# Eight kilobytes of gather scratch turned into a seventh raw buffer and a seventh gather buffer, with one more U tile beside each of two copies

## The chip, the core and the metric

The kernel runs on one core of a Trainium2 chip. That core has a matrix engine (TensorE, PE in the rows below), a vector engine (VectorE, DVE), a scalar engine (ScalarE, ACT), a general engine (GpSimd, POOL) and an engine that mostly issues transfers (SyncE, SP), and it moves data with 16 DMA engines that all of its queues share. The metric is the device time in microseconds of one execution, the median of several runs.

## What is computed

One layer of a streaming encoder on 512 tokens of width 1024: two gated token mixers, then a channel mixer called PEER, in which each token picks 128 of 16384 single-neuron experts (8 heads, 16 experts a head) and adds up their outputs. All of it is float32. The part that this study touches is the second one:

```
q = (t @ w_q).reshape(n_tok, PEER_HEADS, 2, PEER_HALF)
sc = jnp.einsum("thpk,hpnk->thpn", q, sub_keys)          # scores against 2 x 128 keys a head
s_top, i_top = lax.top_k(sc, PEER_TOPK)                  # 16 best of each half, then 16 best sums
...
ue = u_tab[ib]                                           # 128 rows of U for each token
act = jax.nn.gelu(jnp.einsum("phkd,pd->phk", ue, tb))
ve = v_tab[ib]                                           # and 128 rows of V
return jnp.einsum("phk,phkd->pd", gb * act, ve)
```

## The kernel before

The first 360 us are the token mixers (56 weight tiles against all 512 tokens), the next 200 us the queries, scores and top-16 selections. From there PEER is done in two ways at once.

**Tokens 128 to 511 (three token tiles) go the dense way.** The 16384 rows of U are 128 "U tiles" of 128 rows. For each U tile `h_mm` multiplies it with the three token tiles: 24 matmuls of 384 columns, since each float32 operand is split into a high part `hi_u` (made by ACT) and a low part `lo_u` (made by DVE or POOL), and three of the four products are taken. ACT then applies gelu and leaves `hg`, 128 x 384. The gates of the chosen experts are turned into a dense 16384 x 384 matrix by one-hot matmuls (`pg`) that ACT writes to a tile `stg`, 64 KB a partition, one token tile at a time. There is one `stg` buffer. So after token tile 0 and after token tile 1 it is copied out to DRAM (`gd`, four transfers of 2 MB each, line 777), and the one-hot matmuls of the next token tile can only be written once the copy has ended. The third token tile's gates stay in `stg`. In the last phase, iteration i (0 to 127) loads V tile i, reads back the gates `gt` (from `gd`), multiplies them with `hg` to weights `wf`, splits both operands, and adds 18 matmuls of 512 columns to six accumulators (`acc`, lines 831 to 835).

**Tokens 0 to 127 go the sparse way.** POOL gathers 128 rows of U and then 128 rows of V by indirect DMA (`ru`, `rv`, 512 KB each); DVE makes one dot product or one weighted sum of each (lines 373 and 387). The index of a gather is released by ACT (`eix`, line 669), in iteration i of the last phase as a table `pace` says: about three an iteration while U tiles are still multiplied there, three in four iterations afterwards. 8 of the 256 gathers are done before the last phase.

**Where the U tiles are multiplied.** U tiles can run ahead of the last phase: 60 of them do (`nlag = SPILL + AHEAD`), spread by `HST` over the query phase, and then one in each step of the one-hot phase, and `HB` gives the extra steps that follow each copy's start. They are the work that PE has while `stg` is being copied out. 54 of the 60 results do not fit on the chip and are written to DRAM (`hd`, from ACT's queue) and read back as `hr`. The other 68 U tiles are multiplied in the last phase, one an iteration, in iterations 0 to 67; 60 iterations with V alone follow.

**Order.** Up to the last phase each engine's order but SP's is that of the source (`pinned`). In the last phase and on SP a scheduler orders the instructions by its own model of when each can start; only `eix` and gathers are held in source order. SP issues loads in one queue, in order: a load whose buffer is not yet free holds up those behind it. `raw` (U, V, W tiles as loaded, 4 KB a partition) is a ring of RB buffers, and the last four loads, `raw_x2s` (the residual rows that the result is added to), take buffers of the same ring. The gathers alternate between two pools of GR and DR buffers.

```
while t_ < NDT - 1 and len(raws) < RB:      # before a copy: fill the ring
    h_load()
...
for m in range(HB[t_]):                     # U tiles beside the copy
    h_step(lambda: None)
...
gather_release(pace[i], i)                  # ACT: the indices of this iteration's gathers
gather_steps(pace[i], GLEFT)                # POOL: the gathers; DVE: dot products but the last GLEFT
```

Of the kernel before, what the change touches and what calls it, by code (L numbers as in the profile page):

```python
# [35 lines left out]
CGROUPS = [(0, 1, 16), (1, 1, 8), (2, 1, 5), (3, 1, 4), (4, 1, 3), (5, 3, 2), (8, 8, 1)]  # L36
OC = 8
AHEAD = 6
SPILL = 54
OB = 2  # L40
HST = (0,) * 3 + (1,) * 14 + (2,) * 3
HB = (6, 6, 0)
HX = (14, 15, 16)
HPRE = 2
WARM = 28
# [1 line left out]
HPRO2 = 2  # L47
GSTEP = (1, 0, 0)
SB = 3
RB = 6  # L50
DR = 3
GTAIL = 0.5
LATE = 3
FP = (1, 2)
GLEFT = 3
GR = 3
TWO = ("xa", "xc", "cv", "hh", "yb", "gga", "sma")

# [2 lines left out]
def tile_block(ctx: ExitStack, tc: tile.TileContext, x, w_in, vecs, w_ax, w_out, n2row, w_q, skT,  # L61
# [36 lines left out]
    def load(src, name, nsub=None):  # L98
        raw = strm.tile([P, D], F32, tag="raw", name=f"raw_{name}", bufs=RB)
        dst = raw if nsub is None else raw.rearrange("p (a b) -> p a b", a=nsub)  # L100
        sync.dma_start(dst, src)
        return raw
# [273 lines left out]
    def drain(left):  # L376
        while len(dq) > left:
            dq.pop(0)()
# [23 lines left out]
    def h_act(i, pt):  # L402
        g = ha.tile([P, TD], F32, tag="hg", name=f"hg{i}", bufs=AHEAD)
        act.activation(g, pt[:, :TD], AF.Gelu_apprx_tanh)
        if i >= NKEY - SPILL:
            act.dma_start(hd[i - (NKEY - SPILL)], g)
        else:
            hg[i] = g

    def h_get(i):  # L410
        if i not in hg:
            hg[i] = ha.tile([P, TD], F32, tag="hg", name=f"hr{i}", bufs=AHEAD)
            sync.dma_start(hg[i], hd[i - (NKEY - SPILL)])
        return hg[i]

    hd = dram.tile([max(SPILL, 1), P, TD], F32, name="hd")
    hord = list(range(NKEY - SPILL, NKEY)) + list(range(NKEY - SPILL))
    nlag = SPILL + AHEAD
    gd = dram.tile([P, P, TG], F32, name="gd")
# [7 lines left out]
    def h_load():  # L427
        nonlocal hn
        if hn < nlag:
            raws.append((hord[hn], load(uT[hord[hn]], f"u{hord[hn]}")))  # L430
            hn += 1
# [226 lines left out]
    def gather_release(n, i):  # L658
        names, p = [], gpos[0]
        while len(names) < n and p < len(gsched):  # L660
            f, a = gsched[p]
            if f is not gather_w:
                names.append(("ru" if f is gather_u else "rv") + str(a))
            p += 1
        if names:
            t = dp.tile([P, 4], I32, tag="eix", name=f"eix{i}", bufs=4)
            for m, nm in enumerate(names):
                c = int(nm[2:])
                tc.keep_in_program_order(act.activation(t[:, m:m + 1], eall[:, 0, c:c + 1], AF.Copy))  # L669
                gidx[nm] = t[:, m:m + 1]  # L670

    def gather_steps(n, left=0):
        while n > 0 and gpos[0] < len(gsched):
            f, a = gsched[gpos[0]]
            f(a)
            drain(left)
            gpos[0] += 1
            if f is not gather_w:
                n -= 1
# [3 lines left out]
    with ExitStack() as gctx:  # L683
# [51 lines left out]
        def h_step(mid, splits=1):  # L735
            if len(raws) < RB:
                h_load()
            made = []
            while len(made) < splits and len(nxt) + len(made) < SB and raws:
                k_, raw = raws.pop(0)  # L740
                hi = strm.tile([P, D], F32R, tag="hi", name=f"hi_u{k_}", bufs=SB)
                act.activation(hi, raw, AF.Copy)
                made.append((k_, raw, hi))
            mid()
            for k_, raw, hi in made:
                lo = strm.tile([P, D], F32R, tag="lo", name=f"lo_u{k_}", bufs=SB)
                dve.tensor_tensor(lo, raw, hi, op=ALU.subtract)
                nxt.append((k_, (hi, lo), None))
            h_run()
            flush()  # L750
# [4 lines left out]
        for t_ in range(NDT):  # L755
            stg = sp.tile([P, P, P], F32, tag="stg", name=f"stg{t_}", bufs=1)
            for s2 in range(P // OC // 2):
# [8 lines left out]

                if s2 >= 3 and len(raws) < RB:
                    h_load()

                h_step(mid, 0 if t_ and s2 == 0 else 2 if s2 == 3 else 1)  # L770
                gather_steps(GSTEP[(sub // 2) % len(GSTEP)], 2)
            while t_ < NDT - 1 and len(raws) < RB:
                h_load()
            if t_ < NDT - 1:
                for q4 in range(4):
                    sl = slice(q4 * 32, (q4 + 1) * 32)
                    sync.dma_start(gd[sl, :, t_ * P:(t_ + 1) * P].rearrange("i j t -> j i t"), stg[:, sl, :])
            for m in range(HB[t_]):
                h_step(lambda: None)
# [8 lines left out]
    dp = ctx.enter_context(tc.tile_pool(name="dp", bufs=1))  # L788
    rpool.append((dp, DR))
    acc0 = dp.tile([P, D], F32, name="acc0")  # L790
# [49 lines left out]
    for i in range(NKEY):  # L840
# [20 lines left out]
        gather_release(pace[i], i)  # L861
        gather_steps(pace[i], GLEFT)
        if i == NKEY - LATE - 1:
            for j in range(i + 1, NKEY):
                vr[j] = load(v_tab[j * P:(j + 1) * P, :], f"v{j}")
            fgb = dp.tile([P, D], F32, tag="rows", name="fgb", bufs=DR)
            sync.dma_start(fgb, frow.partition_broadcast(P))
            x2s.extend(load(x2d[t], f"x2s{t}") for t in range(NTT))
            x2s.append(dp.tile([P, D], F32, tag="rows", name="junk", bufs=DR))
            drain(0)  # L870
# [51 lines left out]
```

## Time and profile before

| what | value |
|---|---|
| median of 3 runs | 1636.63 us (1634.88 to 1637.17) |
| the profiled execution, its own time | 1635.88 us |
| its span, first to last instruction | 1634.1 us, 1.8 us less than its time |
| PE busy | 1600.7 us, 98% |
| DVE, ACT, POOL busy | 1265.9, 687.7, 522.3 us |
| HBM traffic | 345.17 MB read, 31.59 MB written |
| DMA engines busy in the last phase | 0.93 of their time |
| granted TensorE clock, mean | 0.997 |

A row of a timeline gives the start in us from the span's start, the duration, the engine, the line of the kernel, the operation and the tiles (out<-in, buffer numbers left out), and in brackets how long the engine had been idle and what it had waited for. Matmuls overlap, so what one costs is the distance from its start to the next one's start, not its duration. A row of a stretch gives its ends and length in us, then the busy us and the number of instructions of PE, of PE's weight loads, of DVE, ACT and POOL, then the granted clock as a share of 2.4 GHz, the busy share of the DMA engines and GB/s. Waits are listed as who waited for whom: us in total, how many times, the longest.

### The profile page before, as it was taken

The page shows a single profiled execution, that of the slowest core. Times are in us where ns is not written, and L with a number is a line of the kernel's source. Part 1 is how long each engine was busy: PE and PEld are TensorE (multiplying, and loading weights), DVE is VectorE, ACT ScalarE, POOL GpSimd, SP SyncE. Part 2 cuts the span into 40 slices and gives each one's busy share as a digit, 9 for nine tenths or more (in the row PEclk, how much of TensorE's full clock was granted, in tenths as well). Part 3 has the DMA queues.
Part 4 walks back from the last instruction along what each step waited for, and adds up shares of the span by engine and source line. Part 5 has one row for each costly group of instructions (what it writes and reads, how often), then busy time and mean ns, then how long its engine had stood idle before and what let it go on. Part 6 is the DMA issues. An engine that isn't in the chain of part 4 may idle for free.

```text
span 1634.1 us, 23568 instructions
## 1 busy us (share of the span) xinstructions
PE 1600.7 (98%) x8402; PEld 1413.2 (86%) x8402; DVE 1265.9 (77%) x2404; ACT 687.7 (42%) x1222; POOL 522.3 (32%) x379
## 2 busy tenths in 40 slices
PE   9999999999999999998999999999999999999997
PEld 8888888888899999898989998898999888787775
DVE  6666666636999996767788878888888788877766
ACT  7444444434333454544433333333333333333334
POOL 0000000004788830000144444545444544223331
PEclk9999999999999999999999999999999999999999
DMA  6222222335332357787599989999999999988884
GB/s 227 94 93 94 94 94 96 99 106 180 111 120 101 126 192 221 264 251 232 188 316 333 337 315 329 326 336 319 349 330 335 326 327 348 323 305 297 284 301 144
DMA packets 157878, 378.31 MB, mean 232 GB/s; under 512 B 14016, under 2 KB 78016, under 8 KB 157632
## 3 DMA queue, kind: packets, MB, share of 16 engines
q1 hardware_dynamic: 112544, 229.86, 41.4%
q0 software_dynamic: 36864, 134.23, 23.3%
q10 hardware_dynamic: 8352, 12.72, 2.1%
q8 instruction: 65, 1.06, 0.3%
q14 instruction: 53, 0.43, 0.1%
HBM read 345.17 MB, written 31.59 MB: 231 GB/s over the span
## 4 chain that ended last, share of the span: by engine, by line
PE 59%; DMA 15%; DVE 9%; issue 8%; POOL 4%; ACT 2%; SPq 2%; DVEq 0%; POOLq 0%; ACTq 0%
DMA ru<-in_u_tab_dram,eix 7%; PE pin L149 6%; PE pin L147 6%; PE pin L148 6%; PE ph L147 6%; PE ph L149 6%; PE ph L148 6%; PE acc L832 4%; PE acc L835 4%; PE acc L831 4%; DMA rv<-in_v_tab_dram,eix 4%; POOL rv L364 3%; DMA gd<-stg 2%; PE pq L147 2%; PE pq L149 2%
## 5 line engine op out<-in xcount | busy, mean ns | idle before, releaser
L147 PE MATMUL ph<-a1h,hi_u 128*128 128x384 f32 x1024 | 346.9, 339 | 0.0
L149 PE MATMUL ph<-a1h,lo_u 128*128 128x384 f32 x1024 | 344.2, 336 | 1.8 <-DVE lo_u L108 1.3
L148 PE MATMUL ph<-a1l,hi_u 128*128 128x384 f32 x1024 | 343.3, 335 | 0.0
L832 PE MATMUL acc<-lo_v,wh 128*128 128x512 f32 x768 | 301.7, 393 | 10.7 <-DVE lo_v L108 10.6
L831 PE MATMUL acc<-hi_v,wh 128*128 128x512 f32 x768 | 299.7, 390 | 0.0
L364 POOL DMA_INDIRECT rv<-in_v_tab_dram,eix x128 | 176.8, 1381 | 264.6 <-ACT eix L669 215.0
L835 PE MATMUL acc<-hi_v,wl 128*128 128x512 f32 x768 | 239.0, 390 | 0.0
L364 POOL DMA_INDIRECT ru<-in_u_tab_dram,eix x120 | 164.7, 1372 | 220.1 <-ACT eix L669 176.2
L387 DVE SCALAR_TENSOR_TENSOR acc<-rv,w,acc 128x1024 f32<-128x1024 f32 x128 | 164.5, 1285 | 82.7 <-DMA rv<-in_v_tab_dram,eix 82.5
L107 ACT ACTIVATE hi_v<-raw_v 128x1024 fp32r<-128x1024 f32 x128 | 134.8, 1054 | 190.2 <-PE ph L148 179.1
L373 DVE SCALAR_TENSOR_TENSOR ru<-ru,t 128x1024 f32<-128x1024 f32 x128 | 155.4, 1221 | 62.8 <-DMA ru<-in_u_tab_dram,eix 62.5
L149 PEld LDWEIGHTS ph<-a1h,lo_u 128*128 128x128 f32 x1024 | 192.6, 188 | 3.4 <-DVE lo_u L108 2.6
L148 PEld LDWEIGHTS ph<-a1l,hi_u 128*128 128x128 f32 x1024 | 192.8, 188 | 2.7
L147 PEld LDWEIGHTS ph<-a1h,hi_u 128*128 128x128 f32 x1024 | 192.8, 188 | 2.6
L832 PEld LDWEIGHTS acc<-lo_v,wh 128*128 128x128 f32 x768 | 144.2, 188 | 46.6 <-DVE lo_v L108 18.0
L851 ACT ACTIVATE wh<-wf 128x384 fp32r<-128x384 f32 x128 | 67.0, 524 | 271.3 <-PE acc L832 175.3
L149 PE MATMUL pin<-a1h,lo_in 128*128 128x512 f32 x448 | 174.4, 389 | 0.1
L148 PE MATMUL pin<-a1l,hi_in 128*128 128x512 f32 x448 | 174.4, 389 | 0.0
L147 PE MATMUL pin<-a1h,hi_in 128*128 128x512 f32 x448 | 174.3, 389 | 0.0
L835 PEld LDWEIGHTS acc<-hi_v,wl 128*128 128x128 f32 x768 | 144.1, 188 | 31.2 <-DVE wl L852 0.3
L831 PEld LDWEIGHTS acc<-hi_v,wh 128*128 128x128 f32 x768 | 144.1, 188 | 27.1 <-ACT hi_v L107 0.2
L108 DVE TENSOR_TENSOR lo_v<-raw_v,hi_v 128x1024 fp32r<-128x1024 f32 x128 | 156.0, 1219 | 2.6 <-ACT hi_v L107 2.6
(199 smaller groups left out, 2469.7 us busy)
## 6 DMA issues: line engine op xcount, KB each, us to landing
raw_u<-in_uT_dram SPq DMA_DIRECT2D x128, 512.0 KB, 5.1
raw_v<-in_v_tab_dram SPq DMA_DIRECT2D x128, 512.0 KB, 5.5
raw_in<-in_w_in_dram SPq DMA_DIRECT2D x56, 512.0 KB, 3.3
gd<-stg SPq DMA_DIRECT2D x8, 2048.0 KB, 17.6
gt<-gd SPq DMA_DIRECT2D x128, 128.0 KB, 5.0
hd<-hg ACTq DMA_DIRECT2D x54, 192.0 KB, 2.5
hr<-hd SPq DMA_DIRECT2D x54, 192.0 KB, 5.3
raw_q<-in_w_q_dram SPq DMA_DIRECT2D x16, 512.0 KB, 3.2
```

Source lines behind the costliest of these rows:

```text
L107: act.activation(hi, raw, AF.Copy)
L108: lo_eng.tensor_tensor(lo, raw, hi, op=ALU.subtract)
L147: pe.matmul(pt, wh(k), xh(k), start=start and m == 0, stop=False)
L148: pe.matmul(pt, wh(k), xl(k), start=False, stop=False)
L149: pe.matmul(pt, wl(k), xh(k), start=False, stop=stop and m == n - 1)
L364: ins = pool.indirect_dma_start(out=rows, out_offset=None, in_=tab, in_offset=bass.IndirectOffsetOnAxis(ap=ix, axis=0))
L373: dq.append(lambda: dve.scalar_tensor_tensor(rows, rows, 1.0, t0, op0=ALU.mult, op1=ALU.mult, accum_out=d0[:, n:n + 1]))
L387: dq.append(lambda: dve.scalar_tensor_tensor(acc0, rows, w0[:, n:n + 1], acc0, op0=ALU.mult, op1=ALU.add))
L831: pe.matmul(accs[t][h], wh[:, ts], hi[:, hsl], start=first, stop=False)
L832: pe.matmul(accs[t][h], wh[:, ts], lo[:, hsl], start=False, stop=False)
L835: pe.matmul(accs[t][h], wl[:, ts], hi[:, hsl], start=False, stop=last)
L851: act.activation(wh, wf, AF.Copy)
```

## The change

The scratch that holds the descriptors of indirect transfers is set to 8192 bytes a partition instead of 16384. The room is given to one more `raw` buffer and one more gather buffer, of 4 KB a partition each. Each copy of `stg` gets seven extra U-tile steps beside it instead of six, so that 62 U tiles run ahead of the last phase, 66 run in it, and 56 results go through DRAM. The dot products are written four gathers behind their gather instead of three.

```
-SPILL = 54
+SPILL = 56
-HB = (6, 6, 0)
+HB = (7, 7, 0)
-RB = 6
-DR = 3
+RB = 7
+DR = 4
-GLEFT = 3
+GLEFT = 4
-    nc = _bacc.Bacc("TRN2", target_bir_lowering=False, num_devices=1)
+    nc = _bacc.Bacc("TRN2", target_bir_lowering=False, num_devices=1, dynamic_dma_scratch_size=8192)
```

The U tiles are now taken from number 72 on instead of 74 (then 73, 74, ... 127, 0, 1, ...). ACT at the end of the steps beside the first copy, before; `hg110` is the 37th U tile, and the next instruction is the first write into the emptied gate tile (`stg1`):

```order
L742 ACTIVATE hi_u112_6144<-raw_u112_5968 128x1024
L404 ACTIVATE hg110_6173<-ph110_6148 128x384
L406 DMA hd_2932<-hg110_6173 128x384
L731 ACTIVATE stg1_6176<-pg16_0_6179 128x128x4
L731 ACTIVATE stg1_6176<-pg16_1_6189 128x128x4
```

And the same place now; `hg109` is the 38th:

```order
L404 ACTIVATE hg108_6175<-ph108_6150 128x384
L406 DMA hd_2932<-hg108_6175 128x384
L742 ACTIVATE hi_u111_6180<-raw_u111_5970 128x1024
L404 ACTIVATE hg109_6209<-ph109_6184 128x384
L406 DMA hd_2932<-hg109_6209 128x384
L731 ACTIVATE stg1_6212<-pg16_0_6215 128x128x4
```

One split, one gelu and one store to DRAM have moved in front of that write, and with them 24 matmuls on PE; the same happens at the second copy.

SP at the end of the last phase, before, where `raw_x2s0` is the residual of the first 128 tokens:

```order
L101 DMA raw_v126_15315<-in_v_tab_dram 128x1024
L101 DMA raw_v127_15317<-in_v_tab_dram 128x1024
L844 DMA gt127_15385<-gd_2933 128x256
L867 DMA fgb_15319<-in_frow_dram 128x1024
L101 DMA raw_x2s0_15321<-x2d_75 128x1024
L101 DMA raw_x2s1_15323<-x2d_75 128x1024
```

And now:

```order
L844 DMA gt126_15376<-gd_2933 128x256
L101 DMA raw_v127_15322<-in_v_tab_dram 128x1024
L101 DMA raw_x2s0_15326<-x2d_75 128x1024
L844 DMA gt127_15391<-gd_2933 128x256
L867 DMA fgb_15324<-in_frow_dram 128x1024
```

`raw_x2s0` has moved ahead of two loads, and its buffer is now that of `raw_v121`, seven loads back, where it was that of `raw_v122`.

DVE in the part with V alone, before, at the weighted sum of gather `rv107`, whose index is released in iteration 96 in both kernels:

```order
L108 TENSOR_TENSOR lo_v96_14194<-raw_v96_14191,hi_v96_14193 128x1024
L387 SCALAR_TENSOR_TENSOR acc0_7717<-rv107_14228,w0_2927,acc0_7717 128x1024
L852 TENSOR_TENSOR wl97_14241<-wf97_14239,wh97_14240 128x384
L108 TENSOR_TENSOR lo_v97_14234<-raw_v97_14231,hi_v97_14233 128x1024
L849 TENSOR_TENSOR wf99_14319<-gt99_14317,hr99_14322 128x256
```

And now:

```order
L108 TENSOR_TENSOR lo_v96_14199<-raw_v96_14196,hi_v96_14198 128x1024
L849 TENSOR_TENSOR wf98_14279<-gt98_14277,hr98_14282 128x256
L850 TENSOR_TENSOR wf98_14279<-stg2_7120,hr98_14282 128x128
L387 SCALAR_TENSOR_TENSOR acc0_7785<-rv107_14233,w0_2927,acc0_7785 128x1024
L852 TENSOR_TENSOR wl97_14246<-wf97_14244,wh97_14245 128x384
L108 TENSOR_TENSOR lo_v97_14239<-raw_v97_14236,hi_v97_14238 128x1024
```

The sum stands between the same two V tiles' low parts as before. In the part with U tiles, too, the sum or dot product of a gather of iteration i stands behind `lo_v` of iteration i + 2 in both kernels (all but a handful).

## Rows read from the trace of the kernel before

**Rows 1.** The page: the span, and what each engine is busy.
```profile
span 1634.1 us, 23568 instructions
PE 1600.7 (98%) x8402; PEld 1413.2 (86%) x8402; DVE 1265.9 (77%) x2404; ACT 687.7 (42%) x1222; POOL 522.3 (32%) x379
```

**Rows 2.** Stretches: first copy, after the second copy, last phase with U tiles.
```profile
631.40:668.20 36.80, 34.02 (x228) 33.59 (x227) 18.52 (x16) 9.84 (x14) 0.00 (x0) 1.00 1.01 301
...
747.40:790.00 42.60, 40.44 (x356) 39.09 (x356) 36.87 (x34) 26.94 (x47) 1.68 (x1) 0.94 0.47 166
830.00:1380.00 550.00, 545.84 (x2743) 493.49 (x2742) 458.91 (x631) 212.64 (x467) 265.38 (x199) 1.00 0.93 329
```

**Rows 3.** Waits of PE over the whole span, the two longest.
```profile
PE acc L832 <- DVE lo_v L108: 10.6, 13, 2.2
PE pg L728 <- ACT stg L731: 7.8, 2, 4.4
```

**Rows 4.** PE's timeline at the ends of the two copies.
```profile
665.20 0.22 PE L729 MATMUL pg<-o,oij 128*128 128x128 f16 x1
668.83 0.22 PE L728 MATMUL pg<-o,oij 128*128 128x128 f16 x1 [3.41 <-ACT stg L731]
...
743.46 0.22 PE L729 MATMUL pg<-o,oij 128*128 128x128 f16 x1
748.09 0.26 PE L728 MATMUL pg<-o,oij 128*128 128x128 f16 x1 [4.40 <-ACT stg L731]
...
750.49 0.52 PE L149 MATMUL ph<-a1h,lo_u 128*128 128x384 f32 x1
750.81 0.52 PE L147 MATMUL ph<-a1h,hi_u 128*128 128x384 f32 x1
...
752.41 0.36 PE L149 MATMUL ph<-a1h,lo_u 128*128 128x384 f32 x1
```

**Rows 5.** ACT's timeline beside the first copy.
```profile
641.79 0.49 ACT L404 ACTIVATE hg<-ph 128x384 f32<-128x384 f32 x1 [2.20 <-PE ph L149]
...
645.95 0.49 ACT L404 ACTIVATE hg<-ph 128x384 f32<-128x384 f32 x1 [2.20 <-PE ph L149]
...
668.18 2.06 ACT L731 ACTIVATE stg<-pg 128x512 f32<-128x512 f32 x4 [9.25 <-DMA gd<-stg]
```

**Rows 6.** Waits of DVE for gathers over the whole span.
```profile
DVE acc L387 <- DMA rv<-in_v_tab_dram,eix: 82.5, 50, 5.3
...
DVE ru L373 <- DMA ru<-in_u_tab_dram,eix: 62.5, 51, 2.8
```

**Rows 7.** ACT's timeline at the one iteration with four gathers.
```profile
1152.79 0.47 ACT L669 ACTIVATE eix<-eall 128x1 int32<-128x1 f32 x4
...
1161.05 0.38 ACT L669 ACTIVATE eix<-eall 128x1 int32<-128x1 f32 x3
```

**Rows 8.** SP's timeline near the end.
```profile
1597.70 10.16 SPq L101 DMA_DIRECT2D raw_x2s<-x2d  x3
```

**Rows 9.** DVE's timeline near the end.
```profile
1593.12 1.22 DVE L108 TENSOR_TENSOR lo_v<-raw_v,hi_v 128x1024 fp32r<-128x1024 f32 x1
...
1596.46 1.22 DVE L108 TENSOR_TENSOR lo_v<-raw_v,hi_v 128x1024 fp32r<-128x1024 f32 x1
...
1603.26 1.29 DVE L810 TENSOR_TENSOR raw_x2s<-raw_x2s,acc 128x512 f32<-128x512 f32 x2 [2.25 <-DMA raw_x2s<-x2d]
```

**Rows 10.** PE's timeline near the end.
```profile
1607.57 0.50 PE L832 MATMUL acc<-lo_v,wh 128*128 128x512 f32 x1 [0.63 <-DVE lo_v L108]
...
1614.40 0.50 PE L832 MATMUL acc<-lo_v,wh 128*128 128x512 f32 x1 [1.53 <-DVE lo_v L108]
```

**Rows 11.** The queue that carries the gathers (packets, MB, share); a gather's issue on POOL.
```profile
q0 software_dynamic: 36864, 134.23, 23.3%
...
L364 POOL DMA_INDIRECT rv<-in_v_tab_dram,eix x128 | 176.8, 1381 | 264.6 <-ACT eix L669 215.0
...
rv<-in_v_tab_dram,eix POOLq DMA_INDIRECT x128, 7.3
```

## The prediction, made before the changed kernel ran

> **What bounds the kernel now.** I read the page's first lines, then PE's list of waits, then the stretches, and only then timelines at the few places where PE stops.
>
> PE is busy 1600.7 of 1634.1 us, and no other engine is near that [rows 1]. A busy PE could still be running below its rate, so I take the matmuls' spacing. Beside the copy ACT finishes one U tile every 645.95 − 641.79 = 4.16 us [rows 5], which for 24 matmuls is 0.173 us each. In the last phase with U tiles PE is busy 545.84 of 550 us [rows 2]. The kernel is bound by PE almost throughout; only what PE waits, or runs at a lower clock, can be won.
>
> The waits come to little [rows 3]. Two are the ends of the two copies: PE stands for the one-hot matmuls because ACT cannot evict them into `stg`, 7.8 us together. Thirteen are `lo_v` late on DVE, 10.6 us together. In the timeline the first copy's wait is 668.83 − 665.20 = 3.63 us from start to start, of which 0.06 us is a one-hot matmul's own spacing: 3.57 us lost. The second is 748.09 − 743.46 = 4.63, so 4.57 us lost [rows 4]. After the second the matmuls of 384 columns start 750.81 − 750.49 = 0.32 us apart instead of 0.173, until about 752.41 [rows 4], and that stretch shows a granted clock of 0.94 where the one with the first copy shows 1.00 [rows 2]: PE fell from 2.4 to 1.2 GHz after standing 4.4 us, and not after standing 3.4. Work that took 752.41 − 748.09 = 4.3 us at half rate is worth 2.15, so the lower clock cost about 2.1 us.
>
> What PE stands for is the copy's end: ACT's first eviction after it waited 9.25 us for `gd` [rows 5].
>
> **The change part by part.**
>
> *One more U tile beside each copy.* PE's total work is the same. Each extra step is 4.16 us of PE work taken out of the last phase (iterations 66 and 67 lose their U tile) and put where PE stood. In the last phase it is on the path, since PE is busy there [rows 2]; so 2 × 4.16 = 8.32 us come off there. Beside each copy PE reaches its stop 4.16 us later. If the copy ends when it did, the first wait (3.57 us) is gone and the second (4.57 us) shrinks to 0.41.
>
> Does the copy end when it did? The DMA engines are full while it runs, 1.01 at 301 GB/s [rows 2]. The ring's seventh tile is loaded ahead of the copy, not into it: with seven buffers the ring stays one tile further ahead all along, and the one load between the first and second `gd` waits for the same tile's low part as before. Loads behind the copy stay behind it in SP's queue. What comes in is the extra step's own store of `hg`, 196608 bytes from ACT's queue, which is not behind the copy and shares its engines. Between nothing (it fits a hole) and 196608 bytes at 301 GB/s = 0.65 us, I take 0.4, nearer the upper end because the engines are full.
>
> The Trainium skill, on the page "DMA: Bandwidth & Descriptors", section "Issuing engines are not separate DMA queues", says that transfers from different engines' queues run on the same 16 DMA engines and interleave, which speaks against a store that costs nothing. The share of 1.01 agrees, and by that rule this term would be its upper end, 0.65 us a copy.
>
> First copy: 3.57 + 0.4 − 4.16 is below zero, so all 3.57 us are won (3.51 at the upper end, where 0.06 us of wait stay). Second copy: 4.57 + 0.4 − 4.16 = 0.8 us stay, 3.8 are won (3.5 to 4.2). A wait of 0.8 us is far below the first copy's 3.4, which kept its clock, so the 2.1 us of lower clock are won too. Together 9.5 us (9.1 to 9.8). DVE's extra low part and ACT's extra split lie beside the wait, where DVE is busy 18.5 and ACT 9.8 of 36.8 us [rows 2]; without that cover each would cost about 1.1 us.
>
> *Two more results through DRAM*: two stores, costed above, and two `hr` reads of 0.65 us of DMA in a phase whose DMA share is 0.93 [rows 2]; the two U loads left that phase earlier, 2 × 512 KB, so its traffic falls. Nothing.
>
> *The seventh raw buffer at the end.* `raw_x2s0` now takes the buffer of V tile 121 instead of 122. SP issued it at 1597.70 [rows 8], as the low part that began at 1596.46 ended; the one before it began at 1593.12 [rows 9], so the load moves 3.3 us forward. DVE stood 2.25 us for it at 1603.26 [rows 9], and behind that instruction on DVE stand the weights and low parts of the last V tiles, for which PE then stands 0.63 and 1.53 us [rows 10]. DVE was idle for all of those 2.25 us, so it can use them. PE gains between 0 (another load takes the wait over) and 0.63 + 1.53 = 2.2 us; I take 1.8, since nothing else on DVE waits for a transfer there.
>
> *Dot products four gathers behind.* DVE waits 82.5 + 62.5 = 145 us for gathers [rows 6], and these waits are what makes several of the 13 `lo_v` late. But the order did not move: the scheduler puts a dot product where its model lets it start, and in both kernels that is two V tiles behind its gather's release. So I expect the waits to stay: 0. The bounds are a gain of what the `lo_v` waits leave after the end's two, 10.6 − 2.2 = 8.4 us, and no loss. The seventh gather buffer is idle for the same reason: POOL's wait before a V gather is for the index, 215.0 of 264.6 us [rows 11].
>
> *A denser pace.* 248 gathers are now spread with weights 2 over 66 iterations instead of 68, so 3.08 instead of 3.02 an iteration, and six iterations have four gathers instead of two. At the one in mid-phase the next release came 1161.05 − 1152.79 = 8.26 us later [rows 7], which is 4.16 for the U tile and 4.1 for the 18 matmuls of the V tile, nothing over: no loss. Four more such iterations: 0, at worst 4 × 1.25 us (a dot product) = 5.
>
> *Half the scratch*: 0, for reasons under the rivals.
>
> Sum: −9.5 − 1.8 = −11.3 us against the profiled execution's own 1635.88: 1624.6. That execution lies 0.75 us under the median of the runs, within their spread of 2.3 us. I say **1625**, and 1620 to 1630 for this case: the copies' 9.1 to 9.8, the end's 0 to 2.2, some ±3 for how the small waits of the last phase fall in a new order.
>
> **The rivals.**
>
> *The copy grows with the step.* If the step brings 192 KB of `hg` and also a 512 KB load into the copy, 0.72 MB at 301 GB/s is 2.4 us: the waits stay at 3.57 + 2.4 − 4.16 = 1.8 and 2.8 us, the gain is 1.8 + 1.8 + 2.1 (clock kept), with the end 7.5: 1628.4. For it: the full DMA engines. Against it: SP's order.
>
> *The last phase does not get shorter*, because it runs by its transfers (share 0.93) and not by PE. Then the two steps' 8.3 us are not paid back and the sum is −11.3 + 8.3 = −3.0: 1633, next to no change. For it: the share, 329 GB/s against 301 in the copies. Against it: PE busy 545.84 of 550.
>
> *The dot products do move on the chip*, and 8 us of `lo_v` waits go: 1617. The order speaks against it.
>
> *Slower: half the scratch throttles the gathers.* The trace shows 36864 packets for 256 gathers, 144 each [rows 11] and, at 16 KB, POOL waiting for indices and not for room. It cannot say how many fit in 8 KB. A gather takes 1.4 us on POOL and 7.3 to land, 8.7 together [rows 11]; the phase with U tiles needs one every 8.26 / 3.08 = 2.7 us, so from four places on nothing changes. With three, one comes every 2.9 us, and some 200 gathers lose 0.2 each: +43 us, near 1668. Two places would cost 340 us. Against it: for four gathers to overflow 8 KB, a packet would have to take over 8192 / 9 / 4 = 227 bytes if each of the 16 DMA engines has 8 KB for its nine packets; over 14 bytes if all share one 8 KB. The trace does not decide which.
>
> The Trainium skill, on the same page, "DMA: Bandwidth & Descriptors", gives nine read and nine write descriptors an engine for a transfer to 128 partitions (section "The descriptor swizzle") and 16 bytes a descriptor (section "Terms"). By that (an estimate) a gather takes 144 bytes of each ring and 8192 hold 56: no throttle. The row's 144 packets over 16 engines are nine each, which agrees.
>
> **How the numbers follow.** Forecast case (1620 to 1630) 0.64; the copy grows 0.10; the last phase not shorter 0.12; dot products help 0.06; scratch throttles 0.04; the last 0.04 for losses in the last phase's new order of more than the gain (four-gather iterations, late reads). The range 1618 to 1633.5 leaves out the two slow cases, half of "not shorter" and half of the fast one, 0.17. A change under 0.2%, 3.3 us, cannot be told from none here: faster (under 1633.4) is 0.64 + 0.10 + 0.06 and a part of "not shorter", 0.83; same 0.09; slower 0.08.
>
> **What would show it.** In the new profile: PE's wait for `stg` at the first copy gone, at the second under 1.3 us, and no clock below 1.00 near it; the copy 36.8 us long, within 0.7; the first iteration without a U tile two earlier, the last phase some 8 us shorter; DVE's wait for `raw_x2s` gone; DVE's waits for gathers still 120 to 170 us. It is wrong if the copies lengthen by more than 1 us, if POOL's issues take longer or stand for something new, or if PE's `lo_v` waits grow past 15 us.

## The result, and the profile of the changed kernel

The changed kernel takes 1620.18 us, the median of 6 runs (1619.72 to 1625.24), beside 1636.57 of before in the same runs: 16.4 us less, a ratio of 0.9909 with a 95% interval of 0.9894 to 0.9923. A second set of 6 runs gave 1620.77 beside 1634.73. The forecast was 1625, 11.3 us less. The sign, and the copies as the main source, came out as forecast; the size was too small by 3 to 5 us.

The page's first lines, and PE's waits over the whole span (who waited for whom, us in total, times, longest):

```profile
span 1617.7 us, 23570 instructions
PE 1597.2 (99%) x8402; PEld 1411.7 (87%) x8402; DVE 1265.1 (78%) x2404; ACT 688.3 (43%) x1222; POOL 517.1 (32%) x379
...
PE acc L832 <- DVE lo_v L108: 5.7, 11, 1.2
PE pg L728 <- DVE o L718: 3.1, 4, 0.8
...
PE pg L728 <- ACT stg L731: 1.4, 2, 0.9
```

The span is 16.4 us shorter at the same work. The 7.8 us for `stg` [rows 3] are down to 1.4, and `lo_v` is down from 10.6 to 5.7.

PE at the ends of the two copies:

```profile
669.87 0.22 PE L729 MATMUL pg<-o,oij 128*128 128x128 f16 x1
670.58 0.22 PE L728 MATMUL pg<-o,oij 128*128 128x128 f16 x1 [0.49 <-ACT stg L731]
...
749.52 0.22 PE L729 MATMUL pg<-o,oij 128*128 128x128 f16 x1
750.62 0.22 PE L728 MATMUL pg<-o,oij 128*128 128x128 f16 x1 [0.87 <-ACT stg L731]
```

From start to start the waits are 0.71 and 1.10 us, with the matmul's own 0.06 taken off 0.65 and 1.04, where they were 3.57 and 4.57 [rows 4]. The stretches of both copies and of the 7.1 us behind each (columns as in [rows 2]):

```profile
631.83:669.93 38.10, 38.10 (x253) 37.78 (x252) 17.38 (x15) 11.38 (x16) 0.04 (x1) 1.00 1.01 304
711.49:749.97 38.48, 38.25 (x253) 37.82 (x252) 18.22 (x18) 11.38 (x16) 1.68 (x1) 1.00 1.00 305
669.90:677.00 7.10, 6.61 (x66) 6.33 (x64) 6.81 (x6) 6.11 (x12) 0.00 (x0) 1.00 0.95 365
749.90:757.00 7.10, 6.38 (x61) 6.22 (x61) 5.91 (x6) 6.07 (x12) 0.00 (x0) 1.00 1.00 387
```

The granted clock stays at 1.00 throughout. The first copy has become longer, 38.10 us where it was 36.80 [rows 2]; the second took 747.44 - 709.59 = 37.85 us before, by SP's first issue and ACT's first eviction behind it, and takes 38.48. The profiles of the runs below agree: with six steps the first copy takes 36.8 to 37.0 us in all of them, with seven steps and seven raw buffers 37.6 to 38.1.

SP and DVE near the end:

```profile
1577.42 0.32 SPq L101 DMA_DIRECT2D raw_x2s<-x2d  x1
...
1587.13 1.29 DVE L810 TENSOR_TENSOR raw_x2s<-raw_x2s,acc 128x512 f32<-128x512 f32 x2
```

The residual now is issued 9.7 us ahead of its use (5.6 in [rows 8, 9]), and DVE's wait of 2.25 us for it is gone.

To place the rest, I take the starts of the first and last one-hot matmul, of the last U-tile matmul and of the last V-tile matmul in each profile, and correct for tiles moved: each extra U tile beside a copy takes 4.15 us (24 x 0.173) off the one-hot phase, adds 4.15 + 4.07 (18 x 0.226) to the phase with U tiles, which is that much shorter, and takes 4.07 off the part with V alone. What is then different is waits and clock (single executions, so the two later phases also hold what differs from one execution to the next):

| kernel (one execution each), us | one-hot phase | with U tiles | V alone |
|---|---|---|---|
| before | 205.6 | 579.6 | 256.8 |
| gather_alone | 208.7 | 574.7 | 258.2 |
| ring_alone | 207.6 | 577.5 | 254.4 |
| changed kernel | 197.4 | 576.2 | 251.9 |
| full_again | 197.4 | 577.9 | 251.4 |
| ring_step | 197.1 | 576.3 | 255.1 |

The profile of before is not typical in how its time is split: gather_alone, which takes as long, is 3.1 us longer in the one-hot phase and 3.5 us shorter behind it.

### The profile page after: what moved, and what is told of

The parts are those of the page before. It is cut to its first block, busy times and chain, and to the rows that moved or that the text cites. A ratio compares the mean times of both kernels' runs of the same rounds, so it can differ in the third digit from the quotient of the medians.

```text
span 1617.7 us, 23570 instructions
## 1 busy us (share of the span) xinstructions
PE 1597.2 (99%) x8402; PEld 1411.7 (87%) x8402; DVE 1265.1 (78%) x2404; ACT 688.3 (43%) x1222; POOL 517.1 (32%) x379
## 4 chain that ended last, share of the span: by engine, by line
PE 64%; DMA 12%; DVE 10%; issue 6%; POOL 3%; ACT 2%; SPq 2%; DVEq 0%; ACTq 0%; POOLq 0%
PE pin L149 6%; PE pin L148 6%; PE pin L147 6%; PE ph L147 6%; PE ph L149 6%; PE ph L148 6%; PE acc L832 6%; PE acc L835 5%; PE acc L831 5%; DMA rv<-in_v_tab_dram,eix 5%; DMA ru<-in_u_tab_dram,eix 4%; DMA gd<-stg 2%; PE pq L147 2%; PE pq L149 2%; PE pq L148 2%
## 5 line engine op out<-in xcount | busy, mean ns | idle before, releaser
L364 POOL DMA_INDIRECT rv<-in_v_tab_dram,eix x128 | 171.8, 1342 | 258.0 <-ACT eix L669 211.1
L387 DVE SCALAR_TENSOR_TENSOR acc<-rv,w,acc 128x1024 f32<-128x1024 f32 x128 | 164.7, 1287 | 81.3 <-DMA rv<-in_v_tab_dram,eix 81.2
L373 DVE SCALAR_TENSOR_TENSOR ru<-ru,t 128x1024 f32<-128x1024 f32 x128 | 155.5, 1222 | 52.7 <-DMA ru<-in_u_tab_dram,eix 50.1
```

Source lines behind the costliest of these rows:

```text
L364: ins = pool.indirect_dma_start(out=rows, out_offset=None, in_=tab, in_offset=bass.IndirectOffsetOnAxis(ap=ix, axis=0))
L373: dq.append(lambda: dve.scalar_tensor_tensor(rows, rows, 1.0, t0, op0=ALU.mult, op1=ALU.mult, accum_out=d0[:, n:n + 1]))
L387: dq.append(lambda: dve.scalar_tensor_tensor(acc0, rows, w0[:, n:n + 1], acc0, op0=ALU.mult, op1=ALU.add))
```

## Experiments

Each ran beside the kernel before, whose median in the four sets of runs was 1636.96, 1634.73, 1636.04 and 1638.41 us. The executions of one kernel lie up to 8.5 us from its median, and the four sets ran on chips 3, 15, 3 and 11, so only medians are compared, each first with before in its own set, and of single profiles only what stands at one place.

| label | beside copies | raw buffers | row buffers, lag | scratch | median, us | against before | ratio, 95% |
|---|---|---|---|---|---|---|---|
| ring_alone | 6, 6 | 7 | 3, 3 | 8 KB | 1634.11 | -2.85 | 0.9968 to 0.9993 |
| step_alone | 7, 7 | 6 | 3, 3 | 8 KB | 1642.44 | +5.48 | 1.0017 to 1.005 |
| gather_alone | 6, 6 | 6 | 4, 4 | 8 KB | 1636.55 | -0.41 | 0.9985 to 1.001 |
| ring_step | 7, 7 | 7 | 3, 3 | 8 KB | 1622.79 | -14.17 | 0.9892 to 0.9935 |
| full_again | 7, 7 | 7 | 4, 4 | 8 KB | 1620.77 | -13.96 | 0.9897 to 0.9942 |
| step8_ring7 | 8, 8 | 7 | 4, 4 | 8 KB | 1630.66 | -4.07 | 0.9964 to 0.9993 |
| step8_ring8 | 8, 8 | 8 | 3, 3 | 8 KB | 1620.12 | -14.61 | 0.989 to 0.9927 |
| scratch_1k | 7, 7 | 7 | 4, 4 | 1 KB | 1629.23 | -5.50 | 0.9955 to 0.9987 |
| step8_ring8_gather4 | 8, 8 | 8 | 4, 4 | 4 KB | 1620.80 | -15.24 | 0.9879 to 0.992 |
| scratch_2k | 7, 7 | 7 | 4, 4 | 2 KB | 1619.19 | -16.85 | 0.987 to 0.9912 |
| step_first_copy | 7, 6 | 7 | 3, 3 | 8 KB | 1628.11 | -10.30 | 0.992 to 0.9962 |
| step_second_copy | 6, 7 | 7 | 3, 3 | 8 KB | 1627.26 | -11.15 | 0.9908 to 0.9952 |

All edits are in the constants that the change itself sets; each diff is against the changed kernel.

**The parts, one at a time.** ring_alone:

```
-HB = (7, 7, 0)
-SPILL = 56
-DR = 4
-GLEFT = 4
+HB = (6, 6, 0)
+SPILL = 54
+DR = 3
+GLEFT = 3
```

> Seven raw buffers and 8 KB of scratch, with six U tiles beside each copy, three row buffers and dot products three behind, as before. My theory (the copies' extra step pays 9 us, the seventh raw buffer 2 to 3 us at the end): PE's waits for stg stay near 3.6 and 4.6 us, the wait of DVE for raw_x2s goes, 1634 us (-2 to -3). Rival (the 4.5 us that came on top in the last phase are the ring's, since loads, gates and results come earlier all along it): 1629 to 1630.

Measured -2.85 us: my theory. DVE's wait for `raw_x2s` is gone, and PE's waits for `stg` stay, 3.69 and 4.50 us by the same count:

```profile
669.48 0.22 PE L728 MATMUL pg<-o,oij 128*128 128x128 f16 x1 [3.53 <-ACT stg L731]
...
750.24 0.27 PE L728 MATMUL pg<-o,oij 128*128 128x128 f16 x1 [4.34 <-ACT stg L731]
...
1612.31 0.50 PE L832 MATMUL acc<-lo_v,wh 128*128 128x512 f32 x1 [1.04 <-DVE lo_v L108]
```

The last row is what stays of the two waits of 0.63 and 1.53 us near the end [rows 10]: 1.1 us of the gain stand there, and the rest is not placed.

step_alone:

```
-RB = 7
-DR = 4
-GLEFT = 4
+RB = 6
+DR = 3
+GLEFT = 3
```

> Seven U tiles beside each copy with six raw buffers, 8 KB of scratch, three row buffers, dot products three behind. My theory: the seventh tile has no buffer ahead of the copy, its load stands behind the copy's last transfer in SP's queue (issued near 657 in the trace of before), so PE waits for raw_u or lo_u near 662 to 667 instead of for stg; about half of the copies' gain is left, 1631 us. Rival (the step needs no buffer, the tile's load comes in time): waits as in the changed kernel, 0.7 and 1.0 us, 1627.

Neither: 1642.44, slower than before. The place was right, the price was not. ACT beside the first copy:

```profile
659.14 0.49 ACT L404 ACTIVATE hg<-ph 128x384 f32<-128x384 f32 x1 [2.20 <-PE ph L149]
...
671.70 1.06 ACT L742 ACTIVATE hi_u<-raw_u 128x1024 fp32r<-128x1024 f32 x1 [12.06 <-DMA raw_u<-in_uT_dram]
...
673.61 2.06 ACT L731 ACTIVATE stg<-pg 128x512 f32<-128x512 f32 x4 [0.48 <-DMA raw_u<-in_uT_dram]
```

With six buffers a step's split comes one load short. ACT works in source order here, so it stands for that load until 671.70, with the gelu of a tile that PE had long finished and the gates' eviction queued behind it. The copy is not what it stands for: its last transfer had landed at 668.9 us, 36.8 after the first was issued. PE then stands longer than before, and runs at half clock afterwards (PE's timeline, and the stretch behind the wait):

```profile
669.01 0.34 PE L149 MATMUL ph<-a1h,lo_u 128*128 128x384 f32 x1
676.46 0.29 PE L728 MATMUL pg<-o,oij 128*128 128x128 f16 x1 [7.11 <-DVE o L718]
...
673.60:680.60 7.00, 3.63 (x33) 3.38 (x33) 6.90 (x7) 5.26 (x9) 0.00 (x0) 0.50 0.78 304
```

The list puts PE's wait down to DVE's `o`, the last to come. But DVE had stood for ACT's split, which stood for the load, and `o` comes behind that on DVE:

```profile
672.78 1.22 DVE L747 TENSOR_TENSOR lo_u<-raw_u,hi_u 128x1024 fp32r<-128x1024 f32 x1 [14.59 <-ACT hi_u L742]
...
675.18 1.22 DVE L718 TENSOR_TENSOR o<-oij,g 128x2048 f16<-128x2048 f16 x1
```

The extra step earns nothing without its raw buffer.

gather_alone:

```
-HB = (7, 7, 0)
-SPILL = 56
-RB = 7
+HB = (6, 6, 0)
+SPILL = 54
+RB = 6
```

> A fourth row buffer, dot products four behind and 8 KB of scratch; ring and steps as before. My theory (the scheduler moves no dot product): no change, 1635 to 1638 us, DVE's waits for gathers near 145 us. Rival (the 4.5 us that came on top are the dot products'): 1632 us, PE's waits for lo_v down from 10.6 to about 6.

No change, as expected; PE's waits for `lo_v` are 9.5 us, DVE's for gathers 87.3 + 54.8 = 142.1.

ring_step:

```
-DR = 4
-GLEFT = 4
+DR = 3
+GLEFT = 3
```

> The changed kernel with three row buffers and dot products three behind. My theory: as the changed kernel, 1620 to 1621 us. Rival (the dot products' lag gave the 4.5 us): 1624 to 1625. Second rival (4.5 us are only how small waits of the last phase fall in one order or another): anything between, with other waits at other places.

and the changed kernel once more:

> The changed kernel as it is, once more, to have its size beside the others' in one place. My theory (a gain of 11 to 12 us, and executions of one kernel that lie some 3 us apart to either side): a median between 1620 and 1625 us. Rival (fourth row buffer and longer lag are worth 2 to 4 us once the ring and the steps are there): 1620 again, clear of the 1622.8 without them.

ring_step gave -14.17, the whole change -16.4 and -13.96. The 1622.79 of ring_step lie between my theory (1620 to 1621) and the rival (1624 to 1625), and the 1620.77 of the second set fit both expectations. The means of the 6 runs of ring_step and of the 12 of the whole change are 1622.5 and 1621.1, and the runs of each spread over 8 to 9 us: between nothing and 3 us for the gathers' part, not settled, and at most the smaller share.

**The two copies apart.** The two profiles with six steps at both copies showed something that the profile of before had not: a lower clock behind the first copy as well. So the extra step was given to one copy alone.

```
-HB = (7, 7, 0)
-SPILL = 56
+HB = (7, 6, 0)
+SPILL = 55
```

(and `DR = 3`, `GLEFT = 3`), then the same with `HB = (6, 7, 0)`.

> Seven raw buffers, seven U tiles beside the first copy and six beside the second; three row buffers, dot products three behind, 8 KB of scratch. My theory (the step wins the wait and, in most executions, also a stretch of lower clock of 2 to 2.7 us behind the first copy, which the profiled execution of before did not have): 5 to 6 us below the ring alone, 1627.5 to 1629.5, and a lower clock left behind the second copy only. Rival (behind the first copy the clock seldom falls): 3 us below the ring alone, 1631.

> The same with six U tiles beside the first copy and seven beside the second. My theory: the wait's 3.5 us and a stretch of lower clock of 2.2 to 2.5 us go, 5.5 to 6 us below the ring alone, about 1628, and behind the first copy a lower clock stays. Rival (two steps are needed together, since the last phase is shortened only by whole pairs): less than 3 us below the ring alone.

1628.11 and 1627.26: 6.0 and 6.9 us below ring_alone's 1634.11, as expected, against rivals at 3 (by the differences to before in their own sets 7.5 and 8.3). The two add up to 12.9 or 15.8 us, where both steps together gave 11.3 on top of the ring (ring_step against ring_alone, in one set): each size is known to some 2 us. In the profile of step_second_copy PE stands at the first copy's end exactly as before:

```profile
665.85 0.22 PE L729 MATMUL pg<-o,oij 128*128 128x128 f16 x1
669.45 0.27 PE L728 MATMUL pg<-o,oij 128*128 128x128 f16 x1 [3.37 <-ACT stg L731]
```

and the stretch behind that, 7 us of it, with the one behind the second copy under it, which has its seventh step, and, last, the one behind the second copy in step_first_copy, which has not:

```profile
669.40:676.40 7.00, 6.95 (x36) 6.95 (x36) 4.73 (x5) 4.85 (x9) 0.02 (x1) 0.61 1.00 385
751.00:758.00 7.00, 6.75 (x67) 6.59 (x67) 6.34 (x6) 5.85 (x12) 0.00 (x0) 1.00 1.00 376
```
```profile
749.20:756.20 7.00, 6.96 (x47) 6.81 (x47) 3.59 (x3) 5.03 (x10) 0.00 (x0) 0.77 0.98 365
```

A mean of 0.61 for the 2.4 GHz clock: most of the 7 us ran at 1.2. The same stretch behind the first copy in gather_alone, ring_alone and, last, before:

```profile
668.20:675.20 7.00, 6.59 (x34) 6.59 (x34) 4.65 (x5) 5.21 (x10) 0.00 (x0) 0.57 1.01 377
```
```profile
668.20:675.20 7.00, 5.72 (x35) 5.72 (x35) 4.46 (x5) 5.45 (x10) 0.00 (x0) 0.76 0.98 354
```
```profile
668.20:675.20 7.00, 6.37 (x61) 6.21 (x61) 4.77 (x6) 5.93 (x12) 0.19 (x1) 1.00 0.97 361
```

Three of four executions with that wait (3.5 to 3.7 us in all four) lost the clock behind it; the one I predicted from had kept it. Where it fell, the matmuls of the next 10 us start 1.6 to 2.6 us later in sum than at their usual spacing.

The record of all runs bears this out. Of the 73 executions of the kernel before in the four sets, 65 have a mean granted clock of 0.996 or less; the profiled one has 0.997. The mean of the 73 is 0.9951, that of the 12 executions of the changed kernel 0.9988. The difference of 0.0036 over 1636 us is worth 5.9 us, an upper bound for what the lower clock cost in an average execution, since PE stood during a part of it.

**More of the same.** step8_ring7 and step8_ring8:

```
-HB = (7, 7, 0)
-SPILL = 56
+HB = (8, 8, 0)
+SPILL = 58
```

the second also with `RB = 8`, `DR = 3`, `GLEFT = 3`.

> The changed kernel with eight U tiles beside each copy, still seven raw buffers. My theory (a step beside the copy needs its own raw buffer, or ACT stands for a load that is behind the copy, ahead of the gates' eviction): PE stalls of about 7 us at each copy and a lower clock behind them, 1635 us or more. Rival (six buffers were short by one, and seven are enough for more than seven steps): 1618 to 1620.

> Eight U tiles beside each copy and eight raw buffers, with three row buffers and dot products three behind; 8 KB of scratch. My theory: the waits of 0.65 and 1.03 us left at the copies go, the copies grow by another 0.6 to 1.3 us under the cover of the eighth step, 1619 to 1621, 1 to 2 us below seven and seven. Rival (the copies grow by as much as a step, or two more results through DRAM cost the last phase): 1623 or more.

With seven buffers ACT again stands for a load, and PE stops at both copies, 2.7 and 3.4 us from start to start, with a lower clock behind both stops:

```profile
671.02 1.06 ACT L742 ACTIVATE hi_u<-raw_u 128x1024 fp32r<-128x1024 f32 x1 [7.30 <-DMA raw_u<-in_uT_dram]
...
675.79 0.29 PE L728 MATMUL pg<-o,oij 128*128 128x128 f16 x1 [2.36 <-DVE o L718]
...
675.70:682.70 7.00, 6.40 (x41) 6.14 (x42) 6.90 (x7) 3.41 (x5) 0.00 (x0) 0.51 0.68 270
765.30:772.30 7.00, 6.42 (x44) 6.16 (x45) 6.90 (x7) 3.41 (x5) 0.00 (x0) 0.57 0.67 266
```

The stops were expected at 7 us and the time at 1635 or more. The mechanism holds with stops of under half that size; the time, 1630.66, is 9.9 us over the changed kernel's, where over 14 were expected. With eight buffers the copies' waits for `stg` go and the one-hot phase is 1.1 us shorter (196.3 after the same correction), but the total, 1620.12, is that of the changed kernel within what its runs spread. I had expected the copies to grow by another 0.6 to 1.3 us, and they did not: their last transfers landed 38.0 and 38.1 us after the first issue, in full_again 38.0 and 38.4. With the fourth row buffer and 4 KB of scratch as well:

```
+RB = 8
+HB = (8, 8, 0)
+SPILL = 58
...dynamic_dma_scratch_size=4096)
```

> Eight U tiles beside each copy, eight raw buffers, four row buffers, dot products four behind, 4096 bytes of scratch. My theory (nothing is left at the copies that an eighth step could win, and the gathers' parts are worth under 2 us): 1619 to 1621 us, as with three row buffers. Rival (the fourth row buffer shortens the part with V alone by 3 us, as its length in single profiles suggests): 1617.

1620.80: my theory. Seven steps with seven buffers already have what there is to win at the copies.

**The scratch.** scratch_1k and scratch_2k are the changed kernel with 1024 and 2048 bytes.

> The changed kernel with 1024 bytes of scratch. My theory (up to six gathers are under way and need far less than 8 KB): no change from the changed kernel within 3 us. Rival (a gather needs more than 1024 / 4 = 256 bytes of it): issues on POOL grow from 1.4 us or stand for room, 1650 us or more.

> The changed kernel with 2048 bytes of scratch. My theory (a gather takes 144 bytes, and POOL stands each time the scratch has gone round: at gather 56 and then every 49 with 8 KB, at 113 and 219 with 16 KB): 14 fit, POOL stands at gathers 14, 21, 28 and so on, some 35 times for 0.5 to 1.1 us, 1622 to 1627 us. Rival (what cost 8.5 us with 1 KB is that six gathers under way do not fit): with 2 KB they fit, 1620 to 1622, and no pattern of seven in POOL's stops.

2 KB costs nothing (1619.19). There neither expectation came out whole: the pattern of seven is in POOL's gaps, but the time is under both my 1622 to 1627 and the rival's 1620 to 1622. 1 KB costs 8.5 us against 1620.77 in the same set of runs: my "no change within 3 us" missed, and so did the rival's 1650. POOL does not stand for long anywhere. But counted from the later of the end of ACT's index and of the gather before, to the issue, the gaps show a pattern (gathers counted from 0, one execution each):

| scratch | gaps over 0.45 us from gather 9 on | each |
|---|---|---|
| 16 KB (before) | gathers 113, 219 | 1.1, 1.7 |
| 8 KB (full_again) | 56, 105, 154, 203, 252 | 0.8 to 1.1 |
| 4 KB (step8_ring8_gather4) | 49, 112, 175, 217, 238 | 0.75 |
| 2 KB | 21, 42, 49, 70, 98 and 12 more, all multiples of 7 | 0.59 |
| 1 KB | 12, 15, 18, 21 and so on, 104 of them, from 215 on nearly every one | 0.51 |

Elsewhere the gap is 0.27 to 0.32. Two of those of full_again in POOL's timeline, at gathers 154 and 105:

```profile
1201.73 1.51 POOL L364 DMA_INDIRECT ru<-in_u_tab_dram,eix  x1 [0.78 <-issue]
```
```profile
1068.35 1.50 POOL L364 DMA_INDIRECT rv<-in_v_tab_dram,eix  x1 [0.82 <-DVE lo_u L108]
```

The engines named are chance. The places move with the size of the scratch alone, so I take it that POOL waits there for room in it. In all ten profiles with 8 KB the long gaps stand at 56, 105, 154, 203 or 252 and nowhere else, but few show all five (four have 56, step_first_copy has 252 alone), and at 2 KB 17 of the 35 multiples of 7 from 14 on have one. At each of these places without a long gap, ACT's index had been ready 1.1 us or more before the gather ahead ended: POOL was behind with its issues there. In sum the gaps are 74.5, 75.3 and 77.6 us with 16, 8 and 2 KB, and 97.1 with 1 KB. PE's waits for `lo_v`, with 1 KB and in full_again:

```profile
PE acc L832 <- DVE lo_v L108: 10.0, 14, 1.7
```
```profile
PE acc L832 <- DVE lo_v L108: 7.1, 9, 1.5
```

That is 2.9 of the 6.7 us by which the spans of these two profiles differ (1624.9 and 1618.2). The part with V alone, where nearly every gather has its gap, is 5.4 us longer with 1 KB (256.8 and 251.4). How the rest comes about is open.

The Trainium skill's rule that the prediction cited (page "DMA: Bandwidth & Descriptors", sections "The descriptor swizzle" and "Terms"), by which a gather takes, as an estimate, 144 bytes of each ring, is borne out: 16384 / 144 = 113.8 and 8192 / 144 = 56.9, and the first gaps stand at gathers 113 and 56. So "8192 hold 56" was right. With 4 and 2 KB the first gap by that rule would be at 28 and 14; none shows there, but those that show stand at 28 plus multiples of 21 and at 14 plus multiples of 7.

## Why the prediction was right, and where it was off

**The copies: right in kind, too small.** The seventh step took its 4.15 us off the waits, and the last phase gave back both, since PE bounds it: without the correction the two later phases are 819.8 us together where they were 836.4, and 8.3 of these 16.6 us are the tiles; "the last phase not shorter" is out. The forecast was 3.57 us from the first wait (measured 2.92), 3.8 from the second (3.53) and 2.1 of clock: 9.5. Against the profile of before, the one-hot phase is 205.6 - 197.4 = 8.2 us shorter; against the two siblings with the same waits, which lost the clock at the first copy too, 10.2 and 11.3. The step that failed is the sentence that PE fell to 1.2 GHz "after standing 4.4 us, and not after standing 3.4": that read a rule out of one execution. The first copy's 3.4 us mostly cost the clock too, and in step8_ring7 a stop of 2.7 us did. So the term for clock should have been about 4 us, not 2.1: an estimate from 1.6 to 2.6 us behind each of two copies, under the bound of 5.9 from the mean clocks. step_second_copy shows it behind the first copy; that step_first_copy's 6 us are the wait of 2.9 and the clock together is the likely reading, not separately measured.

**The copy's end: off.** "36.8 us long, within 0.7" and +0.4 a copy came out as +1.3 and +0.6, the first over the 1 us that I had named as a sign of being wrong. The first copy's stretch moved 11.57 MB instead of 11.09: 0.19 MB more in ACT's queue, which is the store I had counted, and 0.29 MB more of SP's queue, U loads that start while the last transfer runs, which I had not. At 301 GB/s the 0.48 MB are 1.6 us. How far these loads made the copy longer, and how far they only filled a longer stretch, is not shown, since the DMA engines are full either way. It cost 0.65 us of wait: 3.57 + 1.3 - 4.16 = 0.7. At the first copy it is the middle between the forecast (0.4) and the rival "the copy grows with the step" (2.4); the second copy's 0.6 is the forecast's upper end.

**The seventh raw buffer: right.** Forecast 1.8, alone 2.85 (0.0007 to 0.0032 of the time, 1.1 to 5.2 us), so the forecast lies inside the interval. What the forecast did not see is that the buffer is the condition of the step: without it the same step costs 5.5 us.

**Dot products and pace: right at 0**, as far as the runs tell: gather_alone -0.4; the waits for gathers are 81.2 + 50.1 = 131.3 us, inside 120 to 170. `lo_v` fell to 5.7, but the same list gives 7.9 in ring_step and 7.1 in full_again, so part of that is one execution's luck.

**Half the scratch: right at 0.** POOL has up to five long gaps instead of two, about 1 us each. That is something new that POOL stands for, which I had named as a sign of being wrong; it cost nothing that can be measured (gather_alone, with 8 KB, -0.41).

**The sum again.** With what the runs showed: waits at the copies 2.9 + 3.5, clock some 4, the ring 2.85: 13.3, beside -13.96 and -16.4 measured and -14.17 without the gathers' part. With the clock at its bound of 5.9 it is 15.2. What is over that in the first set is within the spread of executions, and not settled further.

## What to carry to other kernels

A wait that is near to costing the clock should be priced with it, unless several executions show that it does not: one profile is one draw. A step that fills a wait needs its own buffer ahead of the wait, or an engine that works in order will stand for the load with the very eviction behind it that ends the wait. And once the cover is longer than the wait, more cover brings nothing: eight steps and eight buffers are no better than seven.

## What was unexpected of the hardware

The scratch of indirect transfers can be cut from 16 to 2 KB here without a measurable cost (1619.19 us). At 1 KB the kernel is 8.5 us slower, although at most 6 gathers were ever under way in its profile, from issue to landing. By the 144 bytes above, an estimate, 2 KB hold 14 gathers and 1 KB holds 7. Behind the first round POOL's long gaps stand 106 gathers apart at 16 KB (one distance) and 49, or a multiple, at 8 KB: seven fewer than the 113 and 56 ahead of the first gap. Why seven is not shown.

PE's clock did not follow the length of a stop alone. Behind a wait of 3.6 us it stayed at 2.4 GHz in one profile and fell to 1.2 in three, and it fell behind a stop of 2.7 us in step8_ring7; behind stops of 0.7 and 1.1 us it stayed.
